# Who waits for the last store: SyncE before the closing barrier, or GpSimdE's collecting instruction inside it

## Chip, cores, metric

The kernel runs on one core of one Trainium2 chip. The metric is the device time in microseconds of one execution. The span is the time from the first to the last of the program's own instructions in the profile.

## The reference

```python
# x: (32, 512, 1024) float32
def reference(x):
    max_x = np.max(x, axis=-1, keepdims=True)
    return (max_x.squeeze(-1) + np.log(np.sum(np.exp(x - max_x), axis=-1))).astype(np.float32)
```

It is a log-sum-exp over rows of 1024 numbers, 16384 rows in all. 67 MB are read and 64 KB written.

## The kernel before

The kernel loads the rows in seventeen pieces into a ring in SBUF. ScalarE takes the exponential, ScalarE's accumulator or VectorE adds it up, and a logarithm follows. A branch redoes the work with the maximum subtracted if the sums are out of range, which this input does not need. Two stores write the answer: 112 of the 128 columns early, the last 16 at the end, when the last sum is there.

```python
    nc.scalar.activation(out=res[:, W:NC], in_=sumexp[:, W:NC], func=AF.Ln)
    nc.sync.dma_start(out=out_rows, in_=res[:, 0:W])
    last_store = nc.sync.dma_start(out=out_rest, in_=res[:, W:NC]).ins
    # ... (the check for sums out of range, and the branch)
```

The framework closes the program with a barrier, written here by engine in the order in which each runs it:

```
SyncE         DRAIN that waits for everything: 12 semaphores, the last store's among them
each of four  DRAIN, adds 1 to "gather"; EVENT_SEMAPHORE, waits for "release"
GpSimdE       DRAIN
              EVENT_SEMAPHORE, waits for gather >= 4 and takes 4 off    (the collect)
              EVENT_SEMAPHORE, adds 4 to "release"                      (the release)
              DRAIN
              clears the program's semaphores
              then a second barrier: DRAIN, collect, release
```

In the built program SyncE's twelve conditions are spread over six EVENT_SEMAPHOREs and the DRAIN. A hook that runs when the program is finished puts the store's wait first in the DRAIN's list. The built program then keeps it on the DRAIN itself, where it is waited for last:

```python
    def look_at_store_last(program):
        block, k, drain = next(...)      # SyncE's DRAIN with more than two waits
        store = last_store.sync_info.on_update[0].id
        waits = sorted(drain.sync_info.on_wait, key=lambda wait: wait.id != store)
        assert waits[0].id == store and len(waits) == len(drain.sync_info.on_wait)
        sync = mybir.SyncInfo(on_wait=waits, on_update=list(drain.sync_info.on_update))
        block.instructions[k] = drain.__replace__(sync_info=sync)
```

## Time and profile before

| Kernel before | |
|---|---|
| device time, median of the first 3 runs | 163.57 us (163.52 to 163.73) |
| span of the profiled run | 161.756 us |
| issue of the last store, from the span's start | 159.399 us |
| issue to landing | 1.586 us |
| landing to the start of the collect | 0.104 us |
| landing to the end of the span | 0.771 us |

The last four rows come from the single records of the trace, which have ns resolution: the start of the store's instruction, the sixteenth increment of its semaphore after that (the landing), and the starts of GpSimdE's instructions. "Landing to end" holds the whole closing chain and nothing of the loads. The lines themselves are in the prediction.

### The profile page before, as it was taken

The page shows a single profiled execution, that of the slowest core. Times are in us where ns is not written, and L with a number is a line of the kernel's source. Part 1 is how long each engine was busy: PE and PEld are TensorE (multiplying, and loading weights), DVE is VectorE, ACT ScalarE, POOL GpSimd, SP SyncE. Part 2 cuts the span into 40 slices and gives each one's busy share as a digit, 9 for nine tenths or more (in the row PEclk, how much of TensorE's full clock was granted, in tenths as well). Part 3 has the DMA queues.
Part 4 walks back from the last instruction along what each step waited for, and adds up shares of the span by engine and source line. Part 5 has one row for each costly group of instructions (what it writes and reads, how often), then busy time and mean ns, then how long its engine had stood idle before and what let it go on. Part 6 is the DMA issues. An engine that isn't in the chain of part 4 may idle for free.

```text
span 161.8 us, 221 instructions
## 1 busy us (share of the span) xinstructions
PE 0.8 (0%) x8; PEld 0.3 (0%) x8; DVE 118.5 (73%) x56; ACT 117.2 (72%) x60; POOL 0.2 (0%) x4
## 2 busy tenths in 40 slices
PE   0000000000000000000000000000000000000001
PEld 0000000000000000000000000000000000000000
DVE  0000002999959997299995999999999589799772
ACT  3000069980899609994299924999999999999994
POOL 0000000000000000000000000000000000000000
DMA  7996996997997997998898899889999999999990
GB/s 259 519 519 276 502 519 292 486 519 324 454 519 324 454 519 340 438 519 389 389 519 389 389 519 389 389 389 502 405 389 434 474 389 432 416 428 415 418 368 6
DMA packets 2738, 67.19 MB, mean 415 GB/s; under 512 B 560, under 2 KB 560, under 8 KB 944
## 3 DMA queue, kind: packets, MB, share of 16 engines
q1 hardware_dynamic: 2736, 67.18, 97.0%
q14 instruction: 2, 0.02, 0.0%
HBM read 67.11 MB, written 0.07 MB: 415 GB/s over the span
## 4 chain that ended last, share of the span: by engine, by line
DMA 53%; DVE 35%; ACT 10%; issue 1%; PE 0%
DMA ring<-in_x_dram 53%; DVE sumexp L132 35%; ACT ring L122 9%; ACT ring L120 1%; ACT last_exp L120 0%; PE count L202 0%; DVE fine L203 0%
## 5 line engine op out<-in xcount | busy, mean ns | idle before, releaser
L132 DVE TENSOR_REDUCE sumexp<-ring 128x3 f32<-128x3072 f32 (+5 forms) x21 | 109.5, 5276 | 37.2 <-ACT ring L122 37.2
L122 ACT ACTIVATE ring<-ring 128x3072 f32<-128x3072 f32 (+6 forms) x27 | 100.3, 3763 | 41.4 <-DMA ring<-in_x_dram 41.3
L120 ACT ACTIVATE ring<-ring 128x1024 f32<-128x1024 f32 x14 | 14.6, 1040 | 0.0
L137 DVE SCALAR_TENSOR_TENSOR ring<-ring 128x512 f32<-128x512 f32 x12 | 7.7, 687 | 2.1 <-ACT ring L122 2.1
L120 ACT ACTIVATION_READ_ACCUMULATOR ring<-ring 128x1 f32 x14 | 2.6, 187 | 0.0
L75 ACT ACT_TABLE_LOAD x1 | 1.3, 1283 | 0.8 <-PEq L264 0.8
L102 PE MATMUL count<-far,bad 128*1 128x1 f32 x4 | 0.4, 164 | 158.3 <-DVE clamped L98 158.3
L120 ACT ACTIVATE last_exp<-ring 128x1024 f32<-128x1024 f32 x1 | 1.0, 1027 | 0.0
L137 DVE DVE_READ_ACCUMULATOR ring<-ring 128x1 f32 x12 | 1.0, 83 | 0.0
L76 DVE MEMSET ones<- 128x1 f32 x1 | 0.1, 59 | 0.9 <-PEq L264 0.9
L203 DVE TENSOR_SCALAR fine<-count 1x1 int32<-1x1 f32 x1 | 0.1, 145 | 0.6 <-PE count L202 0.6
L94 DVE TENSOR_SCALAR clamped<-sumexp 128x118 f32<-128x118 f32 (+1 forms) x2 | 0.4, 197 | 0.2
L102 PEld LDWEIGHTS count<-far,bad 128*1 128x1 f32 x4 | 0.2, 81 | 158.4 <-DVE clamped L98 158.4
L98 DVE SCALAR_TENSOR_TENSOR clamped<-clamped,sumexp 128x118 f32<-128x118 f32 (+1 forms) x2 | 0.5, 225 | 0.1
L155 ACT ACTIVATE res<-sumexp 128x112 f32<-128x112 f32 x1 | 0.3, 280 | 0.0
L190 ACT ACTIVATE res<-sumexp 128x16 f32<-128x16 f32 x1 | 0.2, 216 | 0.0
L197 DVE TENSOR_REDUCE bad<-ring 128x1 f32<-128x64 f32 x1 | 0.2, 220 | 0.0
L201 PE MATMUL count<-far,bad 128*1 128x1 f32 x2 | 0.2, 164 | 0.2 <-DVE bad L198 0.2
L202 PE MATMUL count<-ones,sumexp 128*1 128x1 f32 x2 | 0.2, 164 | 0.1
L120 ACT ACTIVATION_READ_ACCUMULATOR last_exp<-ring 128x1 f32 x1 | 0.2, 187 | 0.0
L198 DVE TENSOR_SCALAR bad<-bad 128x1 f32<-128x1 f32 x1 | 0.2, 154 | 0.0
L98 DVE DVE_READ_ACCUMULATOR clamped<-clamped,sumexp 128x1 f32 x2 | 0.2, 82 | 0.0
(7 smaller groups left out, 0.6 us busy)
## 6 DMA issues: line engine op xcount, KB each, us to landing
ring<-in_x_dram SPq DMA_DIRECT2D x1, 6144.0 KB, 28.8
ring<-in_x_dram SPq DMA_DIRECT2D x2, 3072.0 KB, 27.9
ring<-in_x_dram SPq DMA_DIRECT2D x3, 1536.0 KB, 29.2
ring<-in_x_dram SPq DMA_DIRECT2D x1, 4096.0 KB, 27.8
ring<-in_x_dram SPq DMA_DIRECT2D x2, 1024.0 KB, 30.0
ring<-in_x_dram SPq DMA_DIRECT2D x3, 512.0 KB, 25.9
ring<-in_x_dram SPq DMA_DIRECT2D x5, 35.3
out_dram<-res SPq DMA_DIRECT2D x1, 56.0 KB, 8.7
```

What stands on the lines that cost most here:

```text
L75: nc.scalar.preload_act_table_set("natural_log_exp_and_others")
L94: nc.vector.tensor_scalar(out=clamped[:, c0:c1], in0=sumexp[:, c0:c1], scalar1=LOW, scalar2=HIGH, op0=ALU.max, op1=ALU.min,)
L98: counted = nc.vector.scalar_tensor_tensor(out=clamped[:, c0:c1], in0=clamped[:, c0:c1], scalar=0.0, in1=sumexp[:, c0:c1], op0=ALU.bypass, ...
L102: nc.tensor.matmul(count, lhsT=bad[:, i : i + 1], rhs=far, start=i == 0, stop=False)
L120: exp = nc.scalar.activation(out=o, in_=v, func=AF.Exp, accum_out=sums)
L122: exp = nc.scalar.activation(out=v, in_=v, func=AF.Exp)
L132: added = [nc.vector.reduce_sum(out=sums, in_=v, axis=AX.X)]
L137: nc.vector.scalar_tensor_tensor(out=lo, in0=lo, scalar=1.0, in1=ring[:, p + r, H:d], op0=ALU.mult, op1=ALU.add, accum_out=sums[:, r : r + 1],
L155: ln = nc.scalar.activation(out=res[:, 0:W], in_=sumexp[:, 0:W], func=AF.Ln)
L190: nc.scalar.activation(out=res[:, W:NC], in_=sumexp[:, W:NC], func=AF.Ln)
L197: nc.vector.reduce_max(out=bad[:, 3:4], in_=last_row[:, 0, 0 : d // 16], axis=AX.X)
L198: nc.vector.tensor_scalar(out=bad[:, 2:3], in0=bad[:, 3:4], scalar1=LOG_LOW, scalar2=None, op0=ALU.is_lt)
```

## The change

The intent is to take SyncE out of the path between the landing and the barrier. Before, the store wakes SyncE, SyncE goes to the barrier, and its arrival wakes GpSimdE. After, the store wakes GpSimdE, and SyncE has long arrived.

```diff
-        waits = sorted(drain.sync_info.on_wait, key=lambda wait: wait.id != store)
-        assert ...
-        sync = mybir.SyncInfo(on_wait=waits, on_update=list(drain.sync_info.on_update))
+        waits = list(drain.sync_info.on_wait)
+        moved = [wait for wait in waits if wait.id == store]
+        assert len(moved) == 1
+        sync = mybir.SyncInfo(
+            on_wait=[wait for wait in waits if wait.id != store],
+            on_update=list(drain.sync_info.on_update),
+        )
         block.instructions[k] = drain.__replace__(sync_info=sync)
+        k, collect = next(...)           # GpSimdE's first EVENT_SEMAPHORE of the block
+        sync = mybir.SyncInfo(
+            on_wait=moved + list(collect.sync_info.on_wait),
+            on_update=list(collect.sync_info.on_update),
+        )
+        block.instructions[k] = collect.__replace__(sync_info=sync)
```

More of the change, by code (lines that the diff above doesn't have):

```diff
@@ L171, in start_early, with wait_for_store_in_barrier @@
         top.insert(k, first)
-    def look_at_store_last(program):
+    def wait_for_store_in_barrier(program):
         block, k, drain = next(
@@ L181, in look_at_store_last @@
         store = last_store.sync_info.on_update[0].id
-        waits = sorted(drain.sync_info.on_wait, key=lambda wait: wait.id != store)
-        assert waits[0].id == store and len(waits) == len(drain.sync_info.on_wait)
-        sync = mybir.SyncInfo(on_wait=waits, on_update=list(drain.sync_info.on_update))
-        block.instructions[k] = drain.__replace__(sync_info=sync)
+        waits = list(drain.sync_info.on_wait)
[5 more added lines that the diff above has]
+        )
+        block.instructions[k] = drain.__replace__(sync_info=sync)
+        k, collect = next(
+            (k, i) for k, i in enumerate(block.instructions)
+            if i.engine == mybir.EngineType.Pool and isinstance(i, mybir.InstEventSemaphore)
+        )
+        sync = mybir.SyncInfo(
+            on_wait=moved + list(collect.sync_info.on_wait),
+            on_update=list(collect.sync_info.on_update),
+        )
+        block.instructions[k] = collect.__replace__(sync_info=sync)
     nc.at_finalize(start_early)
-    nc.at_finalize(look_at_store_last)
+    nc.at_finalize(wait_for_store_in_barrier)
     nc.scalar.activation(out=res[:, W:NC], in_=sumexp[:, W:NC], func=AF.Ln)
```

## The prediction

> **What bounds the kernel now.** I read the page first (busy shares, the DMA rows, the chain that ended last), then a table of busy time by stretch, then the end of the program: who SyncE waited for, and which closing instructions stand after the last store.
>
> The page, busy shares, queue and chain:
>
> ```profile
> span 161.8 us, 221 instructions
> ...
> DVE  0000002999959997299995999999999589799772
> ACT  3000069980899609994299924999999999999994
> ...
> DMA  7996996997997997998898899889999999999990
> ...
> q1 hardware_dynamic: 2736, 67.18, 97.0%
> ...
> DMA 53%; DVE 35%; ACT 10%; issue 1%; PE 0%
> ```
>
> The busy DMA digits run from the first slice to the last but one, and the queue's packets fill 97.0% of the 16 engines' span. The loads set the time up to about 155 us. The last DMA slice is 0: a tail follows in which nothing moves but the answer. The table by stretch shows that tail (columns: the stretch, its length, busy time and count of PE, PEld, DVE, ACT and POOL, then granted clock, DMA share, GB/s):
>
> ```profile
> 120.00:155.00 35.00, 0.19 (x2) 0.09 (x2) 30.18 (x26) 34.70 (x33) 0.00 (x0) 1.00 1.00 424
> 155.00:159.80 4.80, 0.57 (x6) 0.26 (x6) 3.16 (x14) 4.34 (x7) 0.00 (x0) 1.00 0.52 201
> 159.80:161.00 1.20, 0.00 (x0) 0.00 (x0) 0.00 (x0) 0.00 (x0) 0.00 (x0) 1.00 0.08 7
> 161.00:161.80 0.80, 0.00 (x0) 0.00 (x0) 0.00 (x0) 0.00 (x0) 0.00 (x0) 1.00 0.00 0
> ```
>
> From 159.8 us no engine computes. What passes is one landing (1.2 us) and then a chain of semaphores (0.8 us). The change touches only the joint between these two. The chain of waits on the page ends at 159.54 us with the last arithmetic, so it does not show this joint. SyncE's own waits and the issue list do, with the rows of the closing instructions from 160.95 to 161.2 us below them:
>
> ```profile
> out_dram<-res SPq DMA_DIRECT2D x1, 8.0 KB, 1.6
> ...
> SPq L275 <- DVEq L208: 0.5, 1, 0.5
> SPq L275 <- DMA out_dram<-res: 0.4, 1, 0.4
> ...
> L275 SPq DRAIN  x2: 7/7/7, 161.0 to 161.1; - x2
> L275 POOLq EVENT_SEMAPHORE  x2: 17/17/17, 161.1 to 161.2; - x2
> ```
>
> SyncE waits for the store last, 0.4 us after everything else was in. Then come two of its DRAINs, and only then GpSimdE's two instructions, the collecting one and the releasing one. The single records behind these rows, in ns resolution (start in us, ns long; S is a semaphore's update):
>
> ```
> 160.640       S gather: third of four arrivals (DVE's)
> 160.985       S store: 16th increment, the store has landed
> 161.001   7   SP   DRAIN, waits for the store
> 161.056   7   SP   DRAIN, joins the barrier
> 161.065       S gather: fourth arrival (SP's)
> 161.089  17   POOL collect
> 161.167  17   POOL release
> 161.248  76   POOL DRAIN
> 161.353 113   POOL clears the semaphores
> 161.495  34   POOL DRAIN
> 161.574  17   POOL collect of the second barrier
> 161.652  17   POOL release of the second barrier
> ```
>
> From the landing to the start of the collect there are 161.089 - 160.985 = 104 ns, in four pieces: 16 (SyncE wakes), 55 (from one DRAIN's start to the next one's), 9 (update of the gather semaphore), 24 (GpSimdE wakes). After the collect everything hangs on GpSimdE's own sequence (steps of 78, 81, 105, 142, 79 and 78 ns). The other engines have all come to the second barrier by 161.399, so none of them delays its collect at 161.574. What shifts the first collect shifts the end by as much.
>
> **What the Trainium skill says.** The page "Perfetto Trace Analysis", section "Identifying Dependency Chains", says that an instruction that waits for several engines may get EventSemaphore instructions put ahead of it with the further conditions. The trace agrees: SyncE's closing wait is six EVENT_SEMAPHOREs and a DRAIN that holds the store's wait, the last of all. The same page, section "Sequencer-only Instruction (DRAIN, etc)", says that the profiled start comes when all semaphores are satisfied, and that waiting and propagation lie outside the profiled window. Propagation agrees: a 7 ns DRAIN on the way costs 55 + 9 + 24 ns around it. The start does not agree where an instruction has two waits: SyncE's row for its third EVENT_SEMAPHORE begins at 159.908, when only its first wait was met, and lasts 458 ns, until 22 ns after the second semaphore came at 160.344. So the first wait holds the start and the second lies inside the duration. "DMA: Bandwidth & Descriptors", section "Anatomy of one DMA — SWDGE (gpsimd) path", puts the fixed cost of a DMA near 2.0 us, mostly the confirmation of the write. Here the last 8 KB store lands 1.6 us after its issue; the change leaves that as it is.
>
> **The change part by part.**
>
> Removed: the store's wait on SyncE. Its closing wait then has eleven conditions for twelve; the built program has one SyncE instruction fewer (47 for 48) and as many GpSimdE instructions as before (24). So the collect stays one instruction that waits for the store, then for the four arrivals, and subtracts four. The compute rows of all five engines and the loads are unchanged, but for line numbers.
>
> Moved off the path: SyncE's arrival. Its last wait for something that comes late is the one for VectorE's branch, over at 160.366. In before, three two-wait EVENT_SEMAPHOREs follow in steps of about 60 ns (160.403, 160.465, 160.524), then the DRAINs. In after, two such and two DRAINs follow: about 160.403, 160.465, 160.525 and 160.580, the gather's update 9 ns later, near 160.59. Then VectorE's arrival at 160.640 completes the gather, 345 ns before the landing. I therefore count nothing for SyncE.
>
> Added to the path: GpSimdE wakes on the landing itself. I take its wake as 24 ns, from the two cases in the trace (161.065 to 161.089 here; 0.563 to 0.587 in the opening barrier). The second wait, already met, costs 28 instead of 17 ns, from SyncE's rows with two waits against those with one: 11 ns more. So the collect starts at 160.985 + 0.024 = 161.009 and ends at about 161.037, for 161.106 in before.
>
> Sum: 161.106 - 161.037 = 69 ns gained, or 104 - 24 - 11 = 69. The end of the span goes from 161.756 to about 161.687. The device time is 1.81 us longer than the span in before (163.57 - 161.76); I leave that difference, as it begins when all engines have left the second barrier. 163.57 - 0.07 = 163.50 us, a gain of 0.04%.
>
> **The rivals.**
>
> First: the two-wait collect is resolved the other way round, the arrivals at its start (160.66) and the store inside its duration. Then only some 22 ns follow the landing, as in SyncE's 458 ns row, it ends at 161.007, and the gain is 99 ns: 163.47. For it speaks that hardware need not keep the order of the list; against it, that SyncE's rows of before do keep it.
>
> Second: GpSimdE handles the double wait as two steps, with the 78 ns that lie between its consecutive closing instructions. Then the arrivals are consumed at 161.009 + 0.078 = 161.087, the 104 ns are merely paid in another place, and the time stays at 163.57. For it: GpSimdE's steps (78 ns) are longer than SyncE's (58 to 62 ns). Against it: the unchanged number of instructions, and the ordering, with which the arrivals are long in.
>
> Third: SyncE or another engine becomes the last to arrive. That needs an arrival after 160.985, so 345 ns later than the third one of before; nothing in the change moves VectorE, ScalarE or TensorE, so I give it next to nothing.
>
> Fourth: the loads shift. They are 97% of the span, so 0.1% of them is 0.16 us, over twice the expected gain. The three runs of before spread over 0.21 us (163.52 to 163.73). This is not an effect of the change but it can hide it: in a median of three runs the sign of a 0.07 us gain isn't safe, while its place in the trace is.
>
> **Range and chances.** Centre 163.50 from the 69 ns; the mechanisms span 163.47 to 163.57. The spread of the runs is larger than that, so the range is made from it: about 0.13 us on each side, a little more upward as the runs of before scatter upward. That gives 163.37 to 163.65. Even removing the whole joint, 104 ns, is 0.06%, and a lost step of 78 ns is 0.05%; 2% would be 3.3 us, twice the store's landing time. So within 2%: 0.99, and the rest split evenly for an error in the case as a whole.
>
> **What would show the steps right or wrong.** In the profile after: SyncE's wait for the store is gone, and its two closing DRAINs start near 160.52 and 160.58, before the landing; the gather is complete near 160.64; one GpSimdE EVENT_SEMAPHORE starts 24 ns after the store's last increment and takes about 28 ns (a row of 17/17/28 in place of 17/17/17); the release follows some 90 ns after the collect's start instead of 78; from landing to the end of the span there are about 702 ns in place of 771. A collect that starts near 160.66 and lasts over 300 ns would be the first rival; a third GpSimdE EVENT_SEMAPHORE or a release 156 ns after the collect's start would be the second. Wrong altogether would be a landing that comes later after the store's issue than 1.6 us because GpSimdE waits for it, or a time that moves by more than 0.3 us in all runs.

## The result

| | before | after |
|---|---|---|
| device time, median of 6 runs | 163.60 us (163.52 to 163.73) | 163.59 us (163.51 to 163.83) |
| ratio | | 1.0001 (0.9988 to 1.0014) |
| span of the profiled run | 161.756 us | 162.045 us |
| issue of the last store | 159.399 us | 159.764 us |
| issue to landing | 1.586 us | 1.563 us |
| landing to the collect's start | 104 ns | 24 ns |
| length of the collect | 17 ns | 43 ns |
| landing to the end of the span | 771 ns | 718 ns |

A ratio here is the estimate from the runs of both kernels, with its 95% interval. It is not quite the ratio of the medians quoted, nor that of the plain means.

The device time does not tell the two apart. The profiled run of the changed kernel is even longer by 0.29 us, because the loads brought the last store 0.365 us later; the closing chain is shorter by 53 ns. The page of the changed kernel shows the same bound as before, and its own load pattern of this run:

```profile
span 162.0 us, 220 instructions
...
DMA  7996998999799799699599599999999999999990
...
q1 hardware_dynamic: 2736, 67.18, 96.9%
```

The DMA digits differ from those of before in the middle of the run, though nothing was changed there. Such differences may be what moves the last store by tenths of a microsecond; this was not tested. The count of instructions has gone from 221 to 220: it is SyncE's one EVENT_SEMAPHORE fewer.

SyncE's own waits in the changed kernel, for the closing lines:

```profile
SPq L288 <- PEq L288: 1.0, 2, 0.6
SPq L288 <- DVEq L221: 0.5, 1, 0.5
```

The row "DMA out_dram<-res: 0.4" of before is gone: SyncE no longer waits for the store. It waits for VectorE's branch as before (0.5 us) and then for the release of the barrier (its row under PEq; at the longest 0.6 us, where it had been 0.4). The closing line's instructions from 160.85 to 161.01 us show who arrives:

```profile
L288 SPq DRAIN  x2: 7/7/7, 160.9 to 161.0; - x2
L288 SPq EVENT_SEMAPHORE  x1: 28/28/28, 160.8 to 160.8; - x1
L288 ACTq DRAIN  x1: 8/8/8, 160.9 to 160.9; - x1
L288 DVEq DRAIN  x1: 17/17/17, 161.0 to 161.0; - x1
```

Both of SyncE's DRAINs are over by 160.959, and VectorE's arrival at 161.004 is the fourth; the store lands at 161.327. GpSimdE's closing EVENT_SEMAPHOREs, before (L275) and then after (L288), with the shortest, median and longest duration in ns:

```profile
L275 POOLq EVENT_SEMAPHORE  x4: 17/17/17, 161.1 to 161.7; - x4
```

```profile
L288 POOLq EVENT_SEMAPHORE  x4: 17/17/43, 161.4 to 161.9; - x4
```

One of the four has grown from 17 to 43 ns. It is the collect, with its second wait. The records (start in us, ns long) lead from the landing to the release:

```
161.327       the store has landed
161.351  43   GpSimdE collect: store, then gather >= 4, takes 4 off
161.455  17   GpSimdE release      (128 ns after the landing; before: 182)
162.045       end of the span      (718 ns after the landing; before: 771)
```

### The profile page after: what moved, and what is told of

Read it like the earlier page. It is cut to its first block, busy times and chain, and to the rows that moved or that the text cites. A ratio compares the mean times of both kernels' runs of the same rounds, so it can differ in the third digit from the quotient of the medians.

```text
span 162.0 us, 220 instructions
## 1 busy us (share of the span) xinstructions
PE 0.8 (0%) x8; PEld 0.3 (0%) x8; DVE 118.5 (73%) x56; ACT 117.3 (72%) x60; POOL 0.2 (0%) x4
## 3 DMA queue, kind: packets, MB, share of 16 engines
q1 hardware_dynamic: 2736, 67.18, 96.9%
## 4 chain that ended last, share of the span: by engine, by line
DMA 53%; DVE 35%; ACT 10%; issue 1%; PE 0%
DMA ring<-in_x_dram 53%; DVE sumexp L132 35%; ACT ring L122 9%; ACT ring L120 1%; ACT last_exp L120 0%; PE count L215 0%; DVE fine L216 0%
```

## The experiments

Theory: the closing chain is a fixed row of steps behind the landing. The change cut the hop over SyncE (104 ns from the landing to the collect, now 24) and paid for a second wait on the collect (26 ns), so from the landing on it is worth 80 - 26 = 54 ns by this rounding, 53 as measured, a thirtieth of a per cent. The loads' scatter hides that. Rivals: the time after the span takes the gain back; the profile of the changed kernel was a lucky one; the gain comes from SyncE having less to wait for and not from the place of the wait; the 26 ns come from waiting for a DMA's semaphore.

Eight of the twelve runs that follow (all but the third one of the changed kernel, the second one of the wait on the clearing, the wait on the DRAIN behind the release and the needless second wait) are compared with the same nine runs of the kernel before, four of them with a tenth added. The median of the nine is 163.80 us, for 163.60 in the first rounds. The other four share six runs of it. So the ratios are not independent of one another.

Each experiment edits the same hook. All results were correct, and all kernels still wait for the store before they clear its semaphore and end.

### The changed kernel again

No edit.

> The changed kernel once more, unedited. My theory: the closing chain is a fixed count of steps, and the loads alone scatter. So from the store's landing to the end of the span there are 718 ns again, give or take 5 (before: 771), with the collect starting 24 ns after the landing and taking 43 ns, while the device time stays within 0.1 us of the kernel before and the ratio's interval holds 1. Rival, that the first profile of the changed kernel was a lucky one: the stretch comes out near 771 or scatters by tens of ns.

Landing to end 718 ns, the collect 24 ns after the landing and 43 ns long, as in the first profile. Device time 163.55 us median of 5 (163.43 to 163.64), against 163.8 for the kernel before in its rounds; ratio 0.9986 (0.9972 to 1.0). The chain is thus a fixed quantity. The ratio would mean 0.23 us, over four times what the chain has given, and 0.1 us had been forecast at most, so it was measured once more.

> The changed kernel a third time, to see which of two ratios is chance: 1.0001 with the first result, 0.9986 with the repeat. My theory: the change is worth 53 ns, 0.03%, so the ratio lies near 0.9997 and its interval holds 1; landing to end 718 ns. Rival (the repeat's 0.9986 was real, so something besides the closing chain got 0.2 us shorter): the ratio stays near 0.9986 with an interval below 1.

718 ns again; 163.58 us median of 6 (163.51 to 163.92), ratio 0.9996 (0.9981 to 1.0010). The 0.9986 was not repeated. Three sets of rounds gave 1.0001, 0.9986 and 0.9996: none excludes the 0.9997 that 53 ns come to, and none shows it.

### The two waits in the other order

```diff
-            on_wait=moved + list(collect.sync_info.on_wait),
+            on_wait=list(collect.sync_info.on_wait) + moved,
```

> The collect's two waits in the other order, the arrivals first and the store second. My theory (the first wait in the list holds the start, the second is looked at within the duration): the collect starts 24 ns after the fourth arrival, before the landing, and ends 22 to 40 ns after the landing, so landing to end is 673 to 703 ns, against 718 for the order of the change. Rival (the order is of no account, or the list is turned round): it starts 24 ns after the landing and takes 43 ns, 718 ns to the end. Device time unchanged within 0.1 us in both.

The collect starts 24 ns after the fourth arrival (160.872, for 160.848) and ends 30 ns after the landing (161.236, for 161.206):

```profile
L288 POOLq EVENT_SEMAPHORE  x4: 17/17/364, 160.9 to 161.8; - x4
```

Its 364 ns are a wait shown as duration. The first wait in the list decides the start in the profile; the second is waited for within the instruction. Landing to end is 681 ns, 37 less than with the store first: the same two conditions cost less when the one that comes last stands last in the list. Device time 163.6 us, ratio 0.9990 (0.9975 to 1.0005), not to be told from the others; its median is 0.2 us below that of the kernel before, over the 0.1 us forecast. So the order in the list counts, and the first rival of the prediction describes this kernel and not the one that was asked about.

### The wait further down: on the release

```diff
-        (the collect gets `moved`)
+        other = block.instructions[k + 1]                # the release
+        sync = mybir.SyncInfo(on_wait=moved, on_update=list(other.sync_info.on_update))
+        block.instructions[k + 1] = other.__replace__(sync_info=sync)
```

> The store's wait one step further down, on the instruction with which GpSimdE releases the engines. My theory: what lies ahead of the wait on GpSimdE costs nothing when it is done before the landing, so the release starts 24 ns after the landing, where the kernel before has it 182 ns after, and landing to end is 771 - 182 + 24 = 613 ns. Rival (the gain of the change came from fewer conditions on SyncE and not from the place of the wait): about 718 ns. Device time: 163.44 by my theory, which the scatter may hide.

The release starts 24 ns after the landing and takes 17 ns; the collect had passed 310 ns before the landing. Landing to end: 613 ns, the number expected. SyncE has the same conditions here as in the changed kernel, so it is the place of the wait that counts. Device time 163.54 us, ratio 0.9992 (0.9978 to 1.0005).

### The wait still further down: on the DRAIN, and on the clearing

The same edit with `k + 2` (the DRAIN behind the release) and `k + 3` (the instruction that clears the semaphores).

> The store's wait on GpSimdE's DRAIN between the release and the clearing of the semaphores. My theory: it starts 24 ns after the landing in place of 263, landing to end 771 - 263 + 24 = 532 ns; by the device time about 0.1 us slower than with the wait on the clearing. Rival (a DRAIN that waits costs more than an EVENT_SEMAPHORE that waits): more than 540 ns.

532 ns, as expected: this DRAIN wakes in the same 24 ns. Device time 163.45 us, ratio 0.9986 (0.9968 to 1.0003). Whether it is 0.1 us slower than the wait on the clearing, as forecast, stays open: the two were not run in the same rounds.

> The store's wait on the instruction with which GpSimdE clears the semaphores, three steps behind the collect. My theory: it starts 24 ns after the landing in place of 368, landing to end 771 - 368 + 24 = 427 ns, and the device time is 163.6 - 0.34 = 163.26 us, outside the scatter of the runs (163.5 to 163.8). Rival, that the time after the span takes back what the span gains: the span shortens and the device time stays at 163.6.

428 ns, for 427 expected. GpSimdE's instructions, here of line 289:

```profile
L289 POOLq EVENT_SEMAPHORE  x4: 17/17/17, 160.6 to 161.3; - x4
L289 POOLq DRAIN  x2: 34/55/76, 160.8 to 161.1; - x2
L289 POOLq EVENT_SEMAPHORE_RANGE_CLEAR  x1: 113/113/113, 161.0 to 161.0; - x1
```

Collect and release have moved to 160.6 and 160.7, ahead of the landing at 160.955, and the clearing starts at 160.979. Device time 163.25 us median of 5 (163.17 to 163.44), ratio 0.9973 (0.9960 to 0.9987). The gain shows in the device time, so the time after the span doesn't take it back. That 163.25 is so near the forecast of 163.26 is luck: the forecast started from 163.6 us for the kernel before, which had 163.80 in these rounds. It was run again beside the changed kernel:

> The wait on the clearing of the semaphores once more, beside the changed kernel on one chip. My theory: landing to end 427 to 428 ns, 343 ns less than the kernel before, so a ratio near 0.9979, and 0.29 us below the changed kernel. Rival (the first 0.9973 was mostly chance): a ratio that can't be told from 1.

428 ns again; 163.46 us median of 6 (163.13 to 163.68), ratio 0.9981 (0.9965 to 0.9997). Both intervals lie below 1, and 343 ns of 163.7 us is 0.21%, a ratio of 0.9979, which both hold. From landing to end this version is 343 ns shorter than the kernel before and 290 ns shorter than the changed one. The device time shows the gain over the kernel before. Over the changed kernel it doesn't settle it: the medians of the same rounds are 163.46 and 163.58 us, the means 163.44 and 163.63, for a forecast difference of 0.29 us. The early release lets no engine leave before the store has landed: the second barrier's release comes 323 ns after the landing.

### The wait further up: on GpSimdE's DRAIN ahead of the collect

The same edit with `k - 1`.

> The store's wait one step further up, on the DRAIN with which GpSimdE opens its part of the barrier, ahead of the collect. My theory: what counts is the steps between the wait and the release, whichever engine takes them. The DRAIN starts 24 ns after the landing and the collect follows one GpSimdE step later (79 ns between another DRAIN of it and the collect behind that), so about 103 ns after the landing, as in the kernel before (104): landing to end about 770 ns. So leaving SyncE gains nothing by itself. Rival (SyncE's part, two DRAINs and an update, is what cost): near 718 or below.

The DRAIN starts 24 ns after the landing, but takes 41 ns (as the same DRAIN does in the kernel before) where the one compared with took 34, so the collect starts 109 ns after the landing for the 103 expected, and landing to end is 776 ns: 5 more than before. Device time 163.67 us, ratio 0.9991 (0.9976 to 1.0007). Leaving SyncE gains nothing by itself, and nor does taking a condition from it. The gain of the change is that no further instruction stands between the one that waits for the store and the collect.

### A second wait that has nothing to do with a store

SyncE waits for the store as before; the collect gets a second wait, behind the arrivals, for the semaphore of the first load's slot, met long ago.

```diff
+        met = [wait for wait in waits if wait.id == first_load.sync_info.on_update[0].id]
+        ...
+            on_wait=list(collect.sync_info.on_wait) + met,
```

> The kernel before (SyncE waits for the store) with one more wait on GpSimdE's collect, behind that for the arrivals and met long ago. My theory: the collect with two waits and an update costs 26 ns more than with one wait and an update (43 for 17 ns), whatever the waits are for, so landing to end is 771 + 26 = 797 ns. Rival (the 26 ns come from waiting for a semaphore that a DMA has just raised): 771, or 782 with the 11 ns that SyncE's rows show.

```profile
L286 POOLq EVENT_SEMAPHORE  x4: 17/17/43, 161.1 to 161.7; - x4
```

43 ns again, and landing to end 798 ns, 27 more than before; the collect starts 104 ns after the landing, as in the kernel before. Device time 163.69 us, ratio 1.0002 (0.9984 to 1.0020). So the 26 ns are the price of two waits and an update in one GpSimdE instruction, not of a semaphore that a DMA has just raised. The 11 ns more that the prediction took are from another engine, and for two waits without an update. The update alone does not make the difference, since VectorE has in every profile one instruction with two waits and no update, both waits met over 4 us earlier (here of the kernel before):

```profile
L197 DVEq EVENT_SEMAPHORE  x1: 50/50/50, 158.3 to 158.3; - x1
```

It takes 50 ns, 29 more than VectorE's 21 ns with one wait. So what a second wait adds differs by engine: 11 ns on SyncE and 29 on VectorE without an update, 26 on GpSimdE with one. No run has two waits without an update on GpSimdE.

### Making SyncE slow on purpose

Twenty empty DRAINs go behind SyncE's closing wait, in the kernel before and in the changed one.

```diff
         block.instructions[k] = drain.__replace__(sync_info=sync)
+        for n in range(20):
+            block.instructions.insert(
+                k + 1, drain.__replace__(name=f"I-{90000 + n}", sync_info=None)
+            )
```

> The kernel before with 20 empty DRAINs on SyncE between its wait for the store and its arrival at the barrier. My theory: they lie on the path in full, 20 times 55 to 58 ns = 1100 to 1160 ns, so landing to end is 1870 to 1930 ns and the device time 1.1 to 1.2 us above that of the kernel before. Rival (the time after the span absorbs what the chain loses): the device time stays.

```profile
L279 SPq DRAIN  x22: 7/7/7, 161.0 to 162.1; - x22
```

All 22 DRAINs follow the landing (160.975). From the waiting DRAIN's start (160.992) to that of the last empty one (162.025) are 1033 ns, 52 each; I had expected 55 to 58. Landing to end is therefore 1805 ns and not 1870 to 1930: 1034 more than before. The device time is 164.62 us, 0.60% (0.45 to 0.76) above that of the kernel before, or 0.98 us of 163.79. What lengthens the chain by 1.03 us lengthens the device time by as much within its interval.

> The changed kernel with the same 20 DRAINs on SyncE at the same place. My theory: SyncE starts on them without the store, so some 370 ns of their 1100 to 1160 ns pass before the landing; SyncE then arrives about 780 ns after the landing and the collect ends about 22 to 40 ns after that. Landing to end about 780 + 92 + 589 - 0 = 1460 ns (92 from arrival to release as in the swapped order, 590 from the release to the end), so 0.35 to 0.45 us faster than the kernel before with 20. Rival (SyncE is still on the path before the landing): the same 1870 to 1930 ns as the kernel before with 20.

```profile
L292 POOLq EVENT_SEMAPHORE  x4: 17/17/616, 161.2 to 162.3; - x4
```

The collect starts 25 ns after the landing (161.159) and stands for 616 ns until SyncE arrives (161.769): here again the second wait of the list lies inside the duration, and the collect ends 31 ns after that arrival. Landing to end is 1291 ns, 514 less than in the kernel before with 20 DRAINs. I had expected 1460: the DRAINs were over-sized as above, and SyncE started on them 435 ns ahead of the landing and not 370. Device time 164.22 us, 0.40 us below 164.62. The forecast was 0.35 to 0.45, but it stood on a chain shorter by some 0.4 us, and the chain came out shorter by 0.51; so this hit is partly luck. The means of the four runs each, 164.17 and 164.70, differ by 0.53 us.

> The changed kernel with only 4 such DRAINs on SyncE, 220 to 235 ns. My theory: they are all hidden in the time before the landing (SyncE arrived some 370 to 420 ns ahead of it), so landing to end is 718 ns and the device time unchanged. Rival (SyncE is still on the path): 718 + 225 = 943 ns.

Landing to end 717 ns, with SyncE's arrival at 160.946 the fourth one and the landing at 161.225 us. Four DRAINs are free here, so in the changed kernel SyncE is off the path. Device time 163.67 us, ratio 0.9990 (0.9975 to 1.0006).

### Where the scatter lies

| profiled run | issue of the last store, us | issue to landing, ns | landing to end, ns | device time, us |
|---|---|---|---|---|
| before | 159.399 | 1586 | 771 | 163.55 |
| after | 159.764 | 1563 | 718 | 163.83 |
| after, again | 159.425 | 1612 | 718 | 163.55 |
| after, third | 159.361 | 1641 | 718 | 163.51 |
| wait on the clearing | 159.337 | 1618 | 428 | 163.17 |
| wait on the clearing, again | 159.695 | 1643 | 428 | 163.56 |

The issue of the last store moves by 0.43 us between these runs, the time from issue to landing by 0.08 us, and landing to end not at all for one kernel. A gain in the last column but one can be read to the nanosecond, and in the last column it drowns until it reaches some tenths of a microsecond. The kernel before was profiled only once; the run with a needless second wait repeats its 104 ns from landing to collect. Why the loads take up to 0.43 us more or less was not looked into.

The middle column matters too, because the prediction named a later landing as a sign of being wrong. In all fourteen profiles the first fifteen increments of the last store's semaphore are in by 1441 to 1455 ns after the issue, and the sixteenth alone scatters, from 1563 to 1688 ns. In the three kernels in which SyncE waits for the store it came at 1586, 1589 and 1588 ns; in the eleven profiles in which GpSimdE waits, at 1563 to 1688, 1627 on average. That is some 40 ns later, against a gain of 53. Of the 364 ways to pick three of the fourteen, 22 have a mean as low as that of the three, so it may be chance; no run was made to decide it. From the issue of the store to the end of the span the kernel before took 2357 ns and the changed one 2281, 2330 and 2359. So the shorter chain is shown from the landing on, and a net gain of the changed kernel is not.

## Why the prediction was right

The measured median, 163.59 us, lies in the range of 163.37 to 163.65, and "within 2%" was right. The number alone tests little: the range was made from the scatter of the runs, and no gain at all (163.57 us) lies in it too. The mechanism is tested in the trace, by its steps:

- What bounds the kernel: right. The loads set the time up to the tail in both profiles (97.0% and 96.9% of the queue's engines), and the change touched only the joint.
- SyncE's arrival off the path: right. Predicted were its closing DRAINs near 160.52 and 160.58 and a full gather at 160.64, which is 1.126, 1.181 and 1.241 us after the store's issue; measured were 1.130, 1.188 and 1.240 us. The run with four more DRAINs shows that this time is free.
- The wake of 24 ns on the landing: right, 24 ns in all three profiles of the changed kernel.
- The second wait: the mechanism right, the size off. "28 instead of 17 ns ... 11 ns more" was taken from SyncE's rows; measured were 43 ns, so 26 more, and the release came 104 ns after the collect's start, not "some 90". This is the only term that was mis-sized: 69 ns predicted, 53 ns measured, and 702 ns from landing to end against 718.
- Nothing given back behind the collect or after the span: right. The steps from the release to the end are 589 ns before and 590 after, and the device time exceeds the span by 1.794 and 1.785 us. (The prediction's 1.81 set the median of three runs against the span of one of them.)
- The landing unmoved: open. It came 1.563, 1.612 and 1.641 us after the issue in the changed kernel, for 1.586 before. The second two are later than the prediction's "1.6 us", and whether GpSimdE's waiting has to do with it was not tested. The 2.0 us that the prediction set beside it belong, by the heading of the section, to DMAs issued by GpSimdE; this store is SyncE's, and nothing in the sum rests on it.
- The first rival, the store's wait inside the duration: did not happen, since the list's order decides, as the swapped kernel shows (681 ns, so 90 gained where the rival had 99). The second, two steps of 78 ns: did not happen, the collect is one row. The third, another engine last: did not happen. The fourth, the loads' scatter over the gain: that is what the device time showed. The centre of 163.50 was missed by 0.09 us, and the comparison of the six runs each gives a ratio of 1.0001, with 53 ns (0.0003) inside its interval.

## What to carry to other kernels

At the end of a program a wait costs its place: put the wait for the event that comes last on the last instruction that still has to have it, here the clearing of the semaphores, and let everything that doesn't need it run ahead. Moving a wait from one engine to another gains only the instructions that no longer lie behind it, and a second wait on one instruction has a price (26 ns here; with the later event last in the list the chain was 37 ns shorter). When a change is worth less than the scatter of the runs, read it between two events of one trace, from the landing to the end, and make a large version of it (twenty DRAINs, or the wait at the far end of the chain) to see that the device time follows. Check as well that the earlier event of the two, here the landing, has not moved.

## What the Trainium skill lacked or had wrong

- "Perfetto Trace Analysis", section "Sequencer-only Instruction (DRAIN, etc)": it has the profiled start when all semaphores are satisfied. With two waits in one EVENT_SEMAPHORE the runs show the start at the first of the list, and the wait for the second inside the duration: 364 ns with the arrivals first, 616 ns with SyncE made slow, 458 ns in SyncE's row of the kernel before.
- The same page, section "Identifying Dependency Chains": it says that further conditions may become EventSemaphore instructions, not what conditions on one instruction cost or that their order counts. On GpSimdE one wait and an update took 17 ns and two waits and an update 43 ns; the order with the later event second was 37 ns shorter (681 for 718 ns).
- No page was found that gives the time from step to step in a program's own closing barrier: about 52 ns from one empty SyncE DRAIN to the next, 78 ns from GpSimdE's collect to its release, 24 ns from a semaphore's last increment to GpSimdE's start.
- "DMA: Bandwidth & Descriptors", section "Anatomy of one DMA — SWDGE (gpsimd) path": its fixed cost of near 2.0 us is for DMAs issued by GpSimdE, and no such figure for a store issued by SyncE was found; the last 8 KB store of the profiled runs, issued by SyncE, landed 1.56 to 1.69 us after its issue.
- No page was found that gives the spacing of a small store's sixteen increments: here fifteen came about 12 ns apart, and the sixteenth 113 to 238 ns after the fifteenth.
